# Two-layer stream step: up weights in one tile per 128 features, prepared two stages ahead, and the order of work at the two MLP ends

## The chip, the cores and the metric

The kernel runs on one core of a Trainium2 chip. The metric is device time in microseconds (us) of one execution; the median of several executions is compared, and the rows come from one execution that was recorded with the hardware profiler.

## The reference, cut to what matters

Two layers run over 1056 tokens (1024 of a new stream, 32 of a running one) of 1024 features; layer 0 mixes tokens with a gated recurrence, layer 1 with a short convolution. The change touches the two MLPs alone.

```python
def rmsnorm(x, g):
    return (x * lax.rsqrt(jnp.mean(x * x, axis=-1, keepdims=True) + EPS)) * g
...
    h = h + y                                  # y: the token mixer of layer i
    m = rmsnorm(h, norm_mlp[i])
    h = h + jnp.square(jax.nn.relu(m @ w_up[i])) @ w_down[i]     # 1024 -> 4096 -> 1024
return rmsnorm(h, norm_final), ...
```

## The kernel before, in words

**Numbers.** Activations lie with features on the 128 partitions and tokens in the free dimension. Every operand of a product, activation or weight, is split into a high part (a cast) and a low part (the difference), and a product is three matmuls on TensorE (PE): low times high, high times low, high times high (`mm3`, lines 107 to 110). Weights are fetched by SyncE's (SP) queue into a `raw` tile of 512 KB, cast to `whi` by ScalarE (ACT, L94) and subtracted to `wlo` by VectorE (DVE, L95). There are three raw, four `whi` and four `wlo` buffers. The residual stream is `hT`, eight tiles of 128 x 1056; the normalised input of an MLP is `xh`, `xl`, eight of each.

**One MLP** (`mlp`, L761). The 4096 hidden features are 16 chunks c of 256. `up(c)` takes two weight tiles, makes two halves j of 128 features in three groups of tokens (384, 384 and 288), 72 matmuls a half, and evacuates each half into a tile `u`: relu and scale on DVE (L788), square on ACT (L789). `sums(c)` makes from the two `u` the seven operand parts (B11, B22, Q1, Q2, T3, B21, T4) of a product of Strassen's kind. `down(c, b)` is one half-block of the down projection, for four of the eight tiles of `hT`: its weights are made by `wsums` (fetch, cast L717 and subtraction L718 of three blocks, four additions of weight blocks on GpSimd (POOL), L720, cast L721 and subtraction L722 of the four sums, so two pairs of `whi` and `wlo`); then come seven steps, each twice (p = 0, 1) six matmuls of 264 columns (L809), which accumulate in PSUM tiles a, b and c. A step's result is added to `hT` by DVE (L818); the first and the last step's is first copied out by ACT (L708) and then added once more by POOL (L709). The third and fifth steps accumulate further in tile a, so they wait until what it held has been read.

**Buffers.** `u`, operand parts and `hT` share one pool of 18 tiles (`ft`); PSUM has four tiles of two banks; there are four `st` tiles for the staged copies.

**The order.** The program is written as a list of stages: up(0), sums(0), up(1), down(0, 0), down(0, 1), sums(1), up(2) and so on. The weights of a stage are prepared (fetch, casts, sums) when the stage before it begins. A scheduler at build time turns the written order, the dependences and the free buffers into one order for each engine; on the chip each engine works in its order. In layer 0 the 16th chunk goes through `plain` (ordinary products, evacuated by L835 and the line below) behind down(14, 1); in layer 1 the last two chunks go through `groups` (products for three groups of tokens, 416 columns in the widest, evacuated by L860), so that the final norm can start early. Both read their activations from tiles of `xh` and `xl`, which the last `up` stages still need; so `split` (L180 and L181) fills them behind the last up projection, and only then comes the last `down`.

The stage list before is:

```python
        for c in range(n):                      # n = 15 in layer 0, 14 in layer 1
            stages.append(up(c))
            if c:
                stages += [down(c - 1, 0), down(c - 1, 1)]
            stages.append(lambda c=c: sums(c))
        stages += [up(c) for c in range(n, NFC)]
        rows = [(c, j) for c in range(n, NFC) for j in range(2)]
        stages.append(lambda: [split(k if last else 6 + k, U[c][j]) for k, (c, j) in enumerate(rows)])
        stages += [down(n - 1, 0), down(n - 1, 1)]
        stages += [groups()] if last else [plain(0), plain(1)]
```

Of the kernel before, what the change touches and what calls it, by code (L numbers as in the profile page):

```python
# [35 lines left out]
def trunk_kernel(  # L36
# [93 lines left out]
    def newps():  # L130
        return psum["new"]()
# [471 lines left out]
    def trio():  # L603

        a, b = pt(), pt()
        return a, [a[:, 0], a[:, 1], b[:, 0]]
# [154 lines left out]
    def mlp(layer, nrm, on_final, last):  # L761
        Wu, Wd = wg_up[layer], wg_down[layer]
        U, X = {}, {}
        two = lambda t: t[:, :768].rearrange("p (i c) -> p i c", i=2)
        sq = lambda t: nc.scalar.activation(t, t, AF.Square)

        def up(c):
            def run(wt):
                U[c] = []
                for j in range(2):  # L770
                    first = c == j == 0
                    a, pss = trio()
                    if first:
                        mm_rows(pss, wt, j, xsrc, nrm.scale)
                    else:
                        for g in range(3):
                            sl, n = gsl(g)
                            mm_block(pss[g], n, sl.start, wt, j, xsrc)
                    r = nrm.r
                    spare = last and (c, j) == (NFC - 1, 1)  # L780
                    u = mp.tile([P, NTOK], F32, tag="sq", name="ulast") if spare else ft("u")
                    for d, ps, sl in ((two(u), a[:, :, :384], slice(0, 768)), (u[:, 768:], pss[2][:, :288], slice(768, NTOK))):
                        if c == 0:
                            nc.scalar.activation(d, ps, AF.Relu)
                            nc.vector.tensor_tensor(u[:, sl], u[:, sl], r[:, sl], op=ALU.mult)
                        else:
                            rr = two(r) if sl.start == 0 else r[:, sl]
                            nc.vector.scalar_tensor_tensor(d, ps, 0.0, rr, op0=ALU.max, op1=ALU.mult)  # L788
                        nc.scalar.activation(u[:, sl], u[:, sl], AF.Square)  # L789
                    U[c].append(u)  # L790

            return lambda: wload(Wu, c), run

        def sums(c):
            X[c] = xsums(*U.pop(c))

        def down(c, b):
            def run(w):
                x = X[c]
                ps = [{}, {}]  # L800
                for i, (bank, f, g, start) in enumerate(STEPS):
                    for p in range(2):
                        if start:
                            ps[p][bank] = pt()
                        t = ps[p][bank]
                        (hi, lo), (xhi, xlo) = w(f, p), x[g]
                        for n, (wf, xf) in enumerate(((lo, xhi), (hi, xlo), (hi, xhi))):
                            for q in range(2):
                                nc.tensor.matmul(t[:, q, :QT], wf, xf[:, q * QT : (q + 1) * QT],  # L809
                                                 start=start and n == 0, stop=n == 2, skip_group_check=True)  # L810
                        v = t[:, :, :QT]
                        for r, h, op in TO[i]:
                            d = hT[4 * b + 2 * p + r][:, h * HALF : (h + 1) * HALF]
                            if i in STAGED:
                                st = mp.tile([P, HALF], F32, tag="st", name="st", bufs=4)
                                stage(d, st, v, op)
                            else:
                                nc.vector.tensor_tensor(q2(d), q2(d), v, op=op)  # L818

            return lambda: wsums(Wd[c, b]), run  # L820

        def plain(b):


            def run(wt):
                hi, lo = wt
                for m in range(4 * b, 4 * b + 4):
                    a, pss = trio()
                    cs = slice(m % 4 // 2 * P, (m % 4 // 2 + 1) * P)
                    for g in range(3):  # L830
                        sl, n = gsl(g)
                        for k in range(2):
                            t = BLK[(m % 2, k)]
                            mm3(pss[g][:, :n], hi[:, t, cs], lo[:, t, cs], xh[6 + k][:, sl], xl[6 + k][:, sl], k == 0, k == 1)
                    nc.vector.tensor_tensor(two(hT[m]), two(hT[m]), a[:, :, :384], op=ALU.add)  # L835
                    nc.vector.tensor_tensor(hT[m][:, 768:], hT[m][:, 768:], pss[2][:, :288], op=ALU.add)
                    if m < 6:
                        on_final(m)
                    elif m == 7:
                        on_final(6)  # L840
                        on_final(7)

            return lambda: wsplit(Wd[NFC - 1, b]), run

        def groups():

            n = NFC - 2

            def run(wts):
                for g in range(3):  # L850
                    c0, nt = FGROUPS[g]
                    sl = slice(c0, c0 + nt)
                    for m in range(KT):
                        ps = newps()[:, :nt]
                        cs = slice(m % 4 // 2 * P, (m % 4 // 2 + 1) * P)
                        for k in range(4):
                            hi, lo = wts[k // 2][m // 4]
                            t = BLK[(m % 2, k % 2)]
                            mm3(ps, hi[:, t, cs], lo[:, t, cs], xh[k][:, sl], xl[k][:, sl], k == 0, k == 3)
                        nc.vector.tensor_tensor(hT[m][:, sl], hT[m][:, sl], ps, op=ALU.add)  # L860
                        on_final(g, m)
# [170 lines left out]
    return np.ascontiguousarray(w.reshape(k // 512, 4, P, n // 256, 256).transpose(3, 0, 2, 1, 4))  # L1032


def _blocks(w):


    import numpy as np

    k, n = w.shape  # L1040
    t = w.reshape(k // 256, 2, P, n // 512, 2, 2, P)
    t = t.transpose(0, 3, 2, 5, 1, 4, 6)
    t = np.stack([t[:, :, :, 0, 0], t[:, :, :, 0, 1], t[:, :, :, 1, 1], t[:, :, :, 1, 0]], 3)
    return np.ascontiguousarray(t.reshape(k // 256, n // 512, P, 4, 256))


def _lay(inputs):
# [6 lines left out]
    return {  # L1054
        "x_t": np.ascontiguousarray(np.concatenate([a["x_prompt"][0], a["x_sample"][0]], 0).T),
        "vecs": np.ascontiguousarray(np.concatenate([cols(a[n]) for n in (
            "norm_mix", "norm_mlp", "norm_final", "g_norm_hgrn", "conv_w", "lb_hgrn", "state_conv")], 1)),
        "state_hgrn": np.ascontiguousarray(a["state_hgrn"]),
        "wg_in_hgrn": _grid(a["w_in_hgrn"][0]),
        "wg_out_hgrn": _grid(a["w_out_hgrn"][0]),  # L1060
        "wg_b_conv": _grid(wc[:, :D]),
        "wg_cu_conv": _grid(cu),
        "wg_out_conv": _grid(a["w_out_conv"][0]),
        "wg_up": np.stack([_grid(w) for w in a["w_up"]]),
        "wg_down": np.stack([_blocks(w) for w in a["w_down"]]),
    }

# [29 lines left out]
```

## Time and profile before

| | |
|---|---|
| median of 3 runs | 2478.2 us (2478.15 to 2479.04) |
| profiled execution | 2478.32 us, its span 2476.3 |
| mean granted clock of TensorE | 0.994 of full speed |
| busy, of the span | PE 2416.0 (98%), DVE 1601.4 (65%), ACT 779.9 (31%), POOL 772.3 (31%) |
| DMA | 122 MB, 49 GB/s |

The span is the stretch from the first to the last instruction; the profiled execution's own time is 2.0 us longer. PE is the engine that is almost always busy, so its idle time is what a reader looks for. The first sum-products of the two MLPs start at 668.1 us and 1775.6 us of the span.

### The profile page before, as it was taken

To read this page: it belongs to the slowest core of one execution; us is meant where nothing else is said; L and a number is where in the kernel's file an instruction comes from. 1 tells how busy PE (TensorE), PEld (TensorE's weight loads), DVE (VectorE), ACT (ScalarE), POOL (GpSimd) and SP (SyncE) were. 2 spreads that over 40 slices of the span, in tenths; PEclk is the share of its full clock that TensorE was granted. 3 is DMA by queue.
4 is the path that set the end of the run, shared out by engine and by line. 5 is a ranking of instruction groups with operands and counts; after the bars stand their busy time and mean duration, and the time that the engine had idled before them with its cause. 6 is when DMAs were issued, how large, how long until landed. Compare 5 with 4: busy or idle time off the path is not lost.

```text
span 2476.3 us, 39365 instructions
## 1 busy us (share of the span) xinstructions
PE 2416.0 (98%) x16548; PEld 2376.2 (96%) x16548; DVE 1601.4 (65%) x2384; ACT 779.9 (31%) x1275; POOL 772.3 (31%) x792
## 2 busy tenths in 40 slices
PE   8999999999999999999998999999999999999988
PEld 8999999989999999999998999999999999999987
DVE  8775757553776776767767533244776767767655
ACT  5121212132333333334334111123333333333334
POOL 3110101011253544535545000002244535544323
PEclk9999999999999999999999999999999999999999
DMA  4101010121111111111111111111111111111101
GB/s 149 38 29 47 21 55 21 55 107 35 35 52 43 60 43 43 52 43 52 44 43 60 36 50 52 35 52 45 41 44 43 52 43 53 42 43 60 52 26 71
DMA packets 35760, 121.99 MB, mean 49 GB/s; under 512 B 4336, under 2 KB 7552, under 8 KB 35584
## 3 DMA queue, kind: packets, MB, share of 16 engines
q1 hardware_dynamic: 33632, 113.58, 14.0%
q0 software_dynamic: 1952, 5.92, 0.6%
q8 instruction: 129, 2.11, 0.4%
q14 instruction: 47, 0.39, 0.0%
HBM read 114.09 MB, written 5.39 MB: 48 GB/s over the span
## 4 chain that ended last, share of the span: by engine, by line
PE 85%; DVE 6%; POOL 4%; ACT 3%; issue 3%; DMA 0%; DVEq 0%; SPq 0%; ACTq 0%; POOLq 0%
PE pb L809 18%; PE pb L108 16%; PE pb L109 15%; PE pb L110 15%; POOL raw L720 4%; PE pj L108 4%; PE pj L109 3%; PE pj L110 3%; DVE wlo L722 1%; ACT whi L721 1%; PE v L492 1%; PE v L493 1%; PE v L494 1%; DVE wlo L718 1%; DVE u L788 1%
## 5 line engine op out<-in xcount | busy, mean ns | idle before, releaser
L108 PE MATMUL pb<-xh,wlo 128*128 128x384 f32 (+2 forms) x2640 | 861.4, 326 | 4.3 <-DVE hT L835 4.3
L110 PE MATMUL pb<-xh,whi 128*128 128x384 f32 (+2 forms) x2640 | 854.2, 324 | 0.0
L109 PE MATMUL pb<-xl,whi 128*128 128x384 f32 (+2 forms) x2640 | 854.0, 323 | 0.0
L108 PEld LDWEIGHTS pb<-xh,wlo 128*128 128x128 f32 x2640 | 497.1, 188 | 9.1 <-issue 2.6
L110 PEld LDWEIGHTS pb<-xh,whi 128*128 128x128 f32 x2640 | 497.2, 188 | 0.5
L109 PEld LDWEIGHTS pb<-xl,whi 128*128 128x128 f32 x2640 | 497.3, 188 | 0.3
L709 POOL TENSOR_TENSOR hT<-hT,st 128x528 f32<-128x528 f32 x232 | 404.1, 1768 | 251.3 <-ACT st L708 251.3
L818 DVE TENSOR_TENSOR hT<-hT,pb 128x528 f32<-128x528 f32 x580 | 374.1, 694 | 45.2 <-PE pb L809 41.1
L720 POOL TENSOR_TENSOR raw<-raw 128x256 f32<-128x256 f32 x232 | 205.8, 887 | 510.8 <-DVE wlo L718 497.2
L94 ACT CAST whi<-raw 128x1024 fp32r<-128x1024 f32 (+1 forms) x143 | 149.1, 1045 | 423.6 <-PE pb L110 265.3
L809 PE MATMUL pb<-B,whi 128*128 128x264 f32 x1392 | 226.8, 285 | 0.0
L95 DVE TENSOR_TENSOR wlo<-raw,whi 128x1024 fp32r<-128x1024 f32 (+1 forms) x143 | 182.6, 1280 | 59.6 <-ACT whi L94 59.1
L809 PEld LDWEIGHTS pb<-B,whi 128*128 128x128 f32 x1392 | 193.2, 189 | 0.0
L108 PE MATMUL pj<-xh,wlo 128*128 128x384 f32 (+1 forms) x536 | 177.7, 332 | 6.3 <-ACT xh L183 6.3
L109 PE MATMUL pj<-xl,whi 128*128 128x384 f32 (+1 forms) x536 | 173.5, 324 | 0.0
L110 PE MATMUL pj<-xh,whi 128*128 128x384 f32 (+1 forms) x536 | 173.1, 323 | 0.0
L708 ACT COPY st<-pb 128x528 f32<-128x528 f32 x232 | 136.1, 601 | 117.1 <-PE pb L809 109.7
L788 DVE SCALAR_TENSOR_TENSOR u<-pb,nr 128x768 f32<-128x768 f32 x118 | 80.5, 701 | 137.8 <-PE pb L110 137.8
L809 PE MATMUL pb<-T,whi 128*128 128x264 f32 x928 | 152.2, 286 | 0.0
L809 PE MATMUL pb<-Q,whi 128*128 128x264 f32 x928 | 150.8, 284 | 0.0
L809 PE MATMUL pb<-B,wlo 128*128 128x264 f32 x696 | 141.8, 285 | 0.0
L722 DVE TENSOR_TENSOR wlo<-raw,whi 128x1024 fp32r<-128x1024 f32 x58 | 71.9, 1239 | 107.5 <-ACT whi L721 107.5
(239 smaller groups left out, 3484.8 us busy)
## 6 DMA issues: line engine op xcount, KB each, us to landing
raw<-in_wg_up_dram SPq DMA_DIRECT2D x64, 512.0 KB, 3.6
raw<-in_wg_down_dram SPq DMA_DIRECT2D x64, 512.0 KB, 3.5
raw<-in_wg_in_hgrn_dram SPq DMA_DIRECT2D x31, 512.0 KB, 4.3
raw<-in_wg_cu_conv_dram SPq DMA_DIRECT2D x16, 512.0 KB, 3.5
xk<-in_x_t_dram SPq DMA_DIRECT2D x8, 528.0 KB, 8.2
hT<-in_x_t_dram POOLq DMA_DIRECT2D x8, 528.0 KB, 6.7
raw<-in_wg_out_hgrn_dram SPq DMA_DIRECT2D x8, 512.0 KB, 4.0
raw<-in_wg_b_conv_dram SPq DMA_DIRECT2D x8, 512.0 KB, 3.5
```

The lines of the kernel that those rows point to most:

```text
L94: nc.scalar.copy(hi, raw)
L95: nc.vector.tensor_tensor(lo, raw, hi.bitcast(F32), op=ALU.subtract)
L108: nc.tensor.matmul(ps, wlo, ah, start=start, stop=False)
L109: nc.tensor.matmul(ps, whi, al, start=False, stop=False)
L110: nc.tensor.matmul(ps, whi, ah, start=False, stop=stop)
L708: nc.scalar.copy(q2(st), v)
L709: nc.gpsimd.tensor_tensor(d, d, st, op=op)
L720: nc.gpsimd.tensor_tensor(raw[:, d], raw[:, d], raw[:, o], op=ALU.add)
L722: nc.vector.tensor_tensor(lo2, raw, hi2.bitcast(F32), op=ALU.subtract)
L788: nc.vector.scalar_tensor_tensor(d, ps, 0.0, rr, op0=ALU.max, op1=ALU.mult)
L809: nc.tensor.matmul(t[:, q, :QT], wf, xf[:, q * QT : (q + 1) * QT], start=start and n == 0, stop=n == 2, skip_group_check=True)
L818: nc.vector.tensor_tensor(q2(d), q2(d), v, op=op)
```

## The change

An up projection's weights come in one tile of 512 KB for each half of 128 features (all eight row blocks of the input) in place of two tiles of 256 features by half the rows; the host lays them out so (`_rows`). `up(c)` becomes two stages, `up(c, 0)` and `up(c, 1)`. Weights are prepared two stages ahead in place of one. In layer 0 the two `split` calls stand between down(14, 0) and down(14, 1). In layer 1 down(13, 0) and down(13, 1) stand ahead of the two halves of up(15), and the operands of `groups` go by `gsplit` into `ft` tiles of their own (gh and gl) and not into `xh` and `xl`; in its first group of tokens `groups` multiplies the first three operands of four outputs before it takes the fourth operand.

```diff
@@ mlp
-        def up(c):
+        def up(c, j):
+            m = 2 * c + j
...
+            def prep():
+                rows = lambda t: t.rearrange("p a (b c) -> p (a b) c", c=P)
+                return [rows(t) for t in wsplit(Wu[m])]
...
+        G = []
+
+        def gsplit(u):
+            h, l = [fp.tile([P, NTOK], F32R, tag="ft", name=t) for t in ("gh", "gl")]
+            nc.scalar.copy(h, u)
+            nc.vector.tensor_tensor(l, u, h.bitcast(F32), op=ALU.subtract)
+            G.append((h, l))
+
@@ groups
-                    for m in range(KT):
-                        ps = newps()[:, :nt]
+                    pss = {}
+                    order = [(m, k) for m in range(KT) for k in range(4)]
+                    if g == 0:
+                        order = [(m, k) for m in range(4) for k in range(3)] + [(m, 3) for m in range(4)] + order[16:]
...
-                            mm3(ps, hi[:, t, cs], lo[:, t, cs], xh[k][:, sl], xl[k][:, sl], k == 0, k == 3)
...
+                        gh, gl = G[k]
+                        mm3(pss[m], hi[:, t, cs], lo[:, t, cs], gh[:, sl], gl[:, sl], k == 0, k == 3)
@@ stages
-            stages.append(up(c))
+            stages += [up(c, 0), up(c, 1)]
...
-        stages += [up(c) for c in range(n, NFC)]
-        rows = [(c, j) for c in range(n, NFC) for j in range(2)]
-        stages.append(lambda: [split(k if last else 6 + k, U[c][j]) for k, (c, j) in enumerate(rows)])
-        stages += [down(n - 1, 0), down(n - 1, 1)]
-        stages += [groups()] if last else [plain(0), plain(1)]
+        stages += [up(n, 0), up(n, 1)]
+        if last:
+            stages += [down(n - 1, 0), down(n - 1, 1)]
+            stages.append(lambda: [gsplit(U[n][j]) for j in range(2)])
+            for j in range(2):
+                stages.append(up(n + 1, j))
+                stages.append(lambda j=j: gsplit(U[n + 1][j]))
+            stages.append(groups())
+        else:
+            stages.append(down(n - 1, 0))
+            stages.append(lambda: [split(6 + j, U[n][j]) for j in range(2)])
+            stages += [down(n - 1, 1), plain(0), plain(1)]
...
-        ready = {0: work[0][0]()}
-        k = 0
+        ready = [work[0][0](), work[1][0]()]
...
-            if k + 1 < len(work):
-                ready[k + 1] = work[k + 1][0]()
-            s[1](ready.pop(k))
-            k += 1
+            if len(ready) < len(work):
+                ready.append(work[len(ready)][0]())
+            s[1](ready[work.index(s)])
```

Line numbers shift a little: L788, L789, L818, L835 and L860 become L787, L788, L821, L838 and L878; those up to 761 stay. Three places show how the instructions move. The names end in a running number, and `u`, `pb`, `nr`, `hT` and `raw` are the up result, PSUM, the norm's scale, the residual stream and the fetched weights.

The first place is DVE in a regular cycle of the first MLP, from the evacuation of an up projection into the first half-block of the down projection. Before:

```order
L788 SCALAR_TENSOR_TENSOR u_7686<-pb_7612,nr_6124 128x768
L788 SCALAR_TENSOR_TENSOR u_7686<-pb_7613,nr_6124 128x288
L788 SCALAR_TENSOR_TENSOR u_7765<-pb_7691,nr_6124 128x768
L744 TENSOR_TENSOR B11_8020<-u_7686,B11_8020 128x528
L718 TENSOR_TENSOR wlo_7772<-raw_7770,whi_7771 128x768
L788 SCALAR_TENSOR_TENSOR u_7765<-pb_7692,nr_6124 128x288
L818 TENSOR_TENSOR hT1_5399<-hT1_5399,pb_7804 128x528
L818 TENSOR_TENSOR hT3_5575<-hT3_5575,pb_7812 128x528
L722 TENSOR_TENSOR wlo_7774<-raw_7770,whi_7773 128x1024
L818 TENSOR_TENSOR hT0_5319<-hT0_5319,pb_7784 128x528
L818 TENSOR_TENSOR hT2_5493<-hT2_5493,pb_7794 128x528
```

With the change:

```order
L787 SCALAR_TENSOR_TENSOR u_7686<-pb_7612,nr_6118 128x768
L787 SCALAR_TENSOR_TENSOR u_7686<-pb_7613,nr_6118 128x288
L718 TENSOR_TENSOR wlo_7693<-raw_7691,whi_7692 128x768
L787 SCALAR_TENSOR_TENSOR u_7779<-pb_7705,nr_6118 128x768
L744 TENSOR_TENSOR B11_8020<-u_7686,B11_8020 128x528
L787 SCALAR_TENSOR_TENSOR u_7779<-pb_7706,nr_6118 128x288
L722 TENSOR_TENSOR wlo_7695<-raw_7691,whi_7694 128x1024
L821 TENSOR_TENSOR hT1_5399<-hT1_5399,pb_7810 128x528
L821 TENSOR_TENSOR hT3_5575<-hT3_5575,pb_7818 128x528
L821 TENSOR_TENSOR hT0_5319<-hT0_5319,pb_7790 128x528
L821 TENSOR_TENSOR hT2_5493<-hT2_5493,pb_7800 128x528
```

L718 and L722, which prepare the second half-block's weights, move ahead of the evacuation of the second up half and ahead of all four additions of the half-block; before, L722 stood between them.

The second place is ACT in the same cycle. Before:

```order
L789 ACTIVATE u_7765<-u_7765 128x768
L717 CAST whi_7771<-raw_7770 128x768
L708 COPY st_7791<-pb_7784 128x528
L789 ACTIVATE u_7765<-u_7765 128x288
L708 COPY st_7801<-pb_7794 128x528
L721 CAST whi_7773<-raw_7770 128x1024
L94 CAST whi_7897<-raw_7896 128x1024
```

With the change:

```order
L788 ACTIVATE u_7686<-u_7686 128x768
L717 CAST whi_7692<-raw_7691 128x768
L788 ACTIVATE u_7686<-u_7686 128x288
L743 CAST B11_8020<-u_7686 128x528
L788 ACTIVATE u_7779<-u_7779 128x768
L721 CAST whi_7694<-raw_7691 128x1024
L788 ACTIVATE u_7779<-u_7779 128x288
L708 COPY st_7797<-pb_7790 128x528
L708 COPY st_7807<-pb_7800 128x528
L94 CAST whi_7785<-raw_7784 128x1024
```

The cast L717 now follows the first half's square, and L721 stands ahead of the last square and of both staged copies, where it stood behind them.

The third place is DVE at the end of the second MLP, around the last half-blocks. Before, with `ulast` the last up result:

```order
L788 SCALAR_TENSOR_TENSOR ulast_22387<-pb_22313,nr_16106 128x768
L181 TENSOR_TENSOR xl0_81<-u_22136,xh0_73 128x1056
L788 SCALAR_TENSOR_TENSOR ulast_22387<-pb_22314,nr_16106 128x288
L181 TENSOR_TENSOR xl1_82<-u_22215,xh1_74 128x1056
L181 TENSOR_TENSOR xl2_83<-u_22308,xh2_75 128x1056
L718 TENSOR_TENSOR wlo_22402<-raw_22400,whi_22401 128x768
L181 TENSOR_TENSOR xl3_84<-ulast_22387,xh3_76 128x1056
L818 TENSOR_TENSOR hT1_5399<-hT1_5399,pb_22434 128x528
L818 TENSOR_TENSOR hT3_5575<-hT3_5575,pb_22442 128x528
L818 TENSOR_TENSOR hT0_5319<-hT0_5319,pb_22414 128x528
L722 TENSOR_TENSOR wlo_22404<-raw_22400,whi_22403 128x1024
L818 TENSOR_TENSOR hT2_5493<-hT2_5493,pb_22424 128x528
```

With the change:

```order
L95 TENSOR_TENSOR wlo_22238<-raw_22236,whi_22237 128x1024
L821 TENSOR_TENSOR hT2_5493<-hT2_5493,pb_22328 128x528
L853 TENSOR_TENSOR gl_22473<-u_22138,gh_22472 128x1056
L95 TENSOR_TENSOR wlo_22356<-raw_22354,whi_22355 128x1024
L821 TENSOR_TENSOR hT5_5751<-hT5_5751,pb_22380 128x528
L821 TENSOR_TENSOR hT7_5927<-hT7_5927,pb_22388 128x528
```

The four L181 of the `split` calls and the weight preparation stood ahead of the last sum-product's additions; now the first `gsplit` subtraction (L853) and the weights of up(15) stand among the additions of the two half-blocks, ahead of those for hT5 and hT7.

## Rows read from the trace of the kernel before

**Rows 1.** The page's busy table: busy us, share of the span, instructions of each engine.

```profile
PE 2416.0 (98%) x16548; PEld 2376.2 (96%) x16548; DVE 1601.4 (65%) x2384; ACT 779.9 (31%) x1275; POOL 772.3 (31%) x792
```

**Rows 2.** Waits of PE, whole span: us in total, times, longest us.

```profile
PE pb L809 <- DVE hT L818: 31.6, 29, 5.3
...
PE pb L108 <- DVE hT L835: 4.3, 2, 2.4
...
PE pb L809 <- ACT st L708: 1.0, 1, 1.0
```

**Rows 3.** Waits of PE in 630:1300, 1300:1310, 1700:2380 and 2380:2400.

```profile
PE pb L809 <- DVE hT L818: 12.1, 14, 0.9
...
PE pb L809 <- DVE hT L818: 2.7, 1, 2.7
...
PE pb L809 <- DVE hT L818: 11.4, 13, 0.9
...
PE pb L809 <- DVE hT L818: 5.3, 1, 5.3
```

**Rows 4.** Timeline of one cycle: start, us, instruction, [idle before and its releaser].

```profile
703.84 1.31 DVE L788 SCALAR_TENSOR_TENSOR u<-pb,nr 128x768 f32<-128x768 f32 x2
704.82 1.18 ACT L789 ACTIVATE u<-u 128x768 f32<-128x768 f32 x2 [1.64 <-DVE u L788]
...
711.44 0.81 ACT L717 CAST whi<-raw 128x768 fp32r<-128x768 f32 x1
...
712.29 0.96 DVE L718 TENSOR_TENSOR wlo<-raw,whi 128x768 fp32r<-128x768 f32 x1 [1.02 <-ACT whi L717]
...
712.56 0.30 PE L110 MATMUL pb<-xh,whi 128*128 128x288 f32 x1
...
712.69 0.40 PE L809 MATMUL pb<-B,wlo 128*128 128x264 f32 x2
...
713.33 3.18 POOL L720 TENSOR_TENSOR raw<-raw 128x256 f32<-128x256 f32 x4 [15.76 <-DVE wlo L718]
...
713.62 0.60 ACT L708 COPY st<-pb 128x528 f32<-128x528 f32 x1 [1.36 <-PE pb L809]
...
714.11 0.45 ACT L789 ACTIVATE u<-u 128x288 f32<-128x288 f32 x1
...
715.08 1.44 DVE L818 TENSOR_TENSOR hT<-hT,pb 128x528 f32<-128x528 f32 x2 [1.47 <-PE pb L809]
...
715.62 0.40 PE L809 MATMUL pb<-Q,wlo 128*128 128x264 f32 x2
...
716.54 1.05 ACT L721 CAST whi<-raw 128x1024 fp32r<-128x1024 f32 x1 [1.50 <-POOL raw L720]
...
717.63 1.26 DVE L722 TENSOR_TENSOR wlo<-raw,whi 128x1024 fp32r<-128x1024 f32 x1 [1.11 <-ACT whi L721]
...
719.56 0.51 PE L809 MATMUL pb<-T,wlo 128*128 128x264 f32 x2 [0.85 <-DVE hT L818]
```

**Rows 5.** Chain of waits, three half-blocks' matmuls: start, us, engine, line, count.

```profile
1257.40 14.84 PE pb L809 x120
...
1304.00 16.19 PE pb L809 x120
...
2394.32 16.55 PE pb L809 x114
```

**Rows 6.** Windows: us, busy (x) PE, PEld, DVE, ACT, POOL, granted clock, DMA, GB/s.

```profile
2394.00:2396.00 2.00, 1.69 (x7) 1.69 (x8) 2.00 (x4) 0.00 (x0) 0.00 (x0) 0.50 0.59 180
```

**Rows 7.** Timeline of POOL at the first MLP's end.

```profile
1296.01 4.98 POOL L720 TENSOR_TENSOR raw<-raw 128x256 f32<-128x256 f32 x4 [9.10 <-DVE wlo L718]
```

**Rows 8.** Timeline of DVE at the second MLP's end.

```profile
2379.69 1.26 DVE L181 TENSOR_TENSOR xl<-u,xh 128x1056 fp32r<-128x1056 f32 x1 [0.89 <-ACT xh L180]
```

**Rows 9.** Timeline of DVE in `groups`: additions of two outputs, one after the other.

```profile
2417.72 0.59 DVE L860 TENSOR_TENSOR hT<-hT,pb 128x416 f32<-128x416 f32 x1 [0.41 <-PE pb L110]
...
2419.99 0.59 DVE L860 TENSOR_TENSOR hT<-hT,pb 128x416 f32<-128x416 f32 x1 [0.41 <-PE pb L110]
```

More of the change, by code (lines that the diff above doesn't have):

```diff
@@ L765, in mlp @@
         sq = lambda t: nc.scalar.activation(t, t, AF.Square)
-        def up(c):
+        def up(c, j):
+            m = 2 * c + j
             def run(wt):
[L769 to L774, printed above, removed]
-                    else:
[L776 to L792, printed above, removed]
@@ new lines, in run @@
+                hi, lo = wt
+                a, pss = trio()
+                ks = [(k, g) for k in range(KT) for g in range(3)] if m == 0 else [(k, g) for g in range(3) for k in range(KT)]
+                for i, (k, g) in enumerate(ks):
+                    sl, n = gsl(g)
+                    if m == 0 and i == 3 * (KT - 1):
+                        nrm.scale()
+                    mm3(pss[g][:, :n], hi[:, k], lo[:, k], xh[k][:, sl], xl[k][:, sl], k == 0, k == KT - 1)
+                r = nrm.r
@@ new lines, in run @@
+                u = ft("u")
+                for d, ps, sl in ((two(u), a[:, :, :384], slice(0, 768)), (u[:, 768:], pss[2][:, :288], slice(768, NTOK))):
+                    if c == 0:
+                        nc.scalar.activation(d, ps, AF.Relu)
+                        nc.vector.tensor_tensor(u[:, sl], u[:, sl], r[:, sl], op=ALU.mult)
+                    else:
+                        rr = two(r) if sl.start == 0 else r[:, sl]
+                        nc.vector.scalar_tensor_tensor(d, ps, 0.0, rr, op0=ALU.max, op1=ALU.mult)
+                    nc.scalar.activation(u[:, sl], u[:, sl], AF.Square)
@@ L794, in sums @@
+                U.setdefault(c, []).append(u)
+            def prep():
+                rows = lambda t: t.rearrange("p a (b c) -> p (a b) c", c=P)
+                return [rows(t) for t in wsplit(Wu[m])]
+            return prep, run
         def sums(c):
@@ L852, in run @@
                     sl = slice(c0, c0 + nt)
-                    for m in range(KT):
-                        ps = newps()[:, :nt]
-                        cs = slice(m % 4 // 2 * P, (m % 4 // 2 + 1) * P)
-                        for k in range(4):
-                            hi, lo = wts[k // 2][m // 4]
-                            t = BLK[(m % 2, k % 2)]
-                            mm3(ps, hi[:, t, cs], lo[:, t, cs], xh[k][:, sl], xl[k][:, sl], k == 0, k == 3)
-                        nc.vector.tensor_tensor(hT[m][:, sl], hT[m][:, sl], ps, op=ALU.add)
-                        on_final(g, m)
+                    pss = {}
+                    order = [(m, k) for m in range(KT) for k in range(4)]
+                    if g == 0:
+                        order = [(m, k) for m in range(4) for k in range(3)] + [(m, 3) for m in range(4)] + order[16:]
+                    for m, k in order:
+                        if k == 0:
+                            pss[m] = newps()[:, :nt]
+                        cs = slice(m % 4 // 2 * P, (m % 4 // 2 + 1) * P)
+                        hi, lo = wts[k // 2][m // 4]
+                        t = BLK[(m % 2, k % 2)]
+                        gh, gl = G[k]
+                        mm3(pss[m], hi[:, t, cs], lo[:, t, cs], gh[:, sl], gl[:, sl], k == 0, k == 3)
+                        if k == 3:
+                            nc.vector.tensor_tensor(hT[m][:, sl], hT[m][:, sl], pss[m], op=ALU.add)
+                            on_final(g, m)
             return lambda: [[wsplit(Wd[n + c, b]) for b in range(2)] for c in range(2)], run
@@ L1032, in _grid, with _rows @@
     return np.ascontiguousarray(w.reshape(k // 512, 4, P, n // 256, 256).transpose(3, 0, 2, 1, 4))
+def _rows(w):
+    import numpy as np
+    k, n = w.shape
+    return np.ascontiguousarray(w.reshape(k // P, P, n // P, P).transpose(2, 1, 0, 3).reshape(n // P, P, k // 256, 256))
 def _blocks(w):
@@ L1063, in _lay @@
         "wg_out_conv": _grid(a["w_out_conv"][0]),
-        "wg_up": np.stack([_grid(w) for w in a["w_up"]]),
+        "wg_up": np.stack([_rows(w) for w in a["w_up"]]),
         "wg_down": np.stack([_blocks(w) for w in a["w_down"]]),
```

## The prediction

> **What bounds the kernel now.** The busy table comes first: TensorE (PE) works 2416.0 us, 98% of the span of 2476.3, and no other engine passes 65% [rows 1]. An edit that keeps the matmuls, as this one does, can win only what PE loses: idle time, and time at its lower clock. So the next view is the table of PE's waits. Its largest line is the sum-product matmul of L809 waiting for the VectorE (DVE) addition of L818, 31.6 us in 29 waits, the longest 5.3; then L809 waiting for the staged copy of L708, 1.0, and L108 waiting for L835 of `plain`, 4.3 in two [rows 2]. Cut by stretch, the 29 fall apart: 14 of 12.1 us in the first MLP, 13 of 11.4 in the second, each at most 0.9, and one long one at each MLP's end, 2.7 and 5.3 [rows 3].
>
> The timeline of one cycle shows where the 0.87 (23.5 / 27) comes from. A cycle is an up projection of one chunk, two half-blocks of sum-products (seven steps each) and the sums. The last up matmul starts at 712.56, the first sum-product at 712.69, the third step at 715.62, so a step takes about 1.47. The weights of the second half-block are prepared while the first runs: cast L717 at 711.44, subtraction L718, four GpSimd (POOL) additions of 3.18 in all, cast L721 at 716.54, subtraction L722 until 718.89. In DVE's order L722 stands ahead of the L818 additions that free bank a, so PE's fifth step starts at 719.56 after 0.85 idle, where 718.71 was possible [rows 4]. What ends last is the weight preparation, through a queue; DVE is not short of time.
>
> The long stalls cost twice. In the chain of waits a half-block's 120 matmuls that went undisturbed took 14.84, those behind the 2.7 us stall 16.19, and 114 behind the 5.3 us stall 16.55 [rows 5]. The window from 2394.00 has a granted clock of 0.50, that is 1.2 of 2.4 GHz, after PE had stood still for over 5 us [rows 6]. At the full pace 114 matmuls need 114 x 14.84 / 120 = 14.10, so the lower clock costs 16.19 - 14.84 = 1.35 and 16.55 - 14.10 = 2.45.
>
> **The change part by part.** Matmuls, weight transfers, casts and subtractions keep their number and size: a chunk still has two weight tiles of 512 KB, now one for each half, and four `gsplit` pairs stand for four `split` pairs. Nothing is priced there; SP's queue issues the same transfers, one stage earlier, and a raw tile stays held by its own preparation alone.
>
> *The regular cycle, 27 times.* The second half-block's weights are now made during the second up half. Let the first sum-product again start at 712.69. L717 follows the first half's evacuation and squares, which in the old trace (for the second half) begin at 703.84 and 704.82 and take 1.31 and 1.18 [rows 4]; with 0.81 for L717 and 0.96 for L718 the latter ends near 707.3 or 708. The POOL additions take 3.18 where POOL is alone, 4.98 in the slowest row I read [rows 4, 7]: done by 710.5 to 713. L721 then wants the hi buffer that the second up half's last matmul still reads, which ends at 712.56 + 0.30 = 712.86. So L721 runs from 712.9 to 713.95 instead of from 716.54.
>
> Two things now stand behind it. On ACT: the last Square (0.45) and the staged copies (0.60 each). The first copy, which wants step 1's output, ends at 713.95 + 0.45 + 0.60 = 715.0 at the latest, 714.6 if the Square slips ahead; the third step, which accumulates into the same bank, starts at 715.62. A slack of 0.6 or more. On DVE: L722, 713.95 to 715.2, then the two additions of bank b (1.44 for both, to 716.65), then the first of bank a, 0.72, to 717.4. The fifth step wants it at 718.71: a slack of 1.3. So the bubble goes with nothing in its place: 27 x 0.87 = **23.5 us**. What is late next is nothing on PE's path in the first half-block. In the second, DVE has what it had before without its L718 and L722; L94 and L95 of the next up half move in there, one tile at a time instead of two, beside 10 us of matmuls in each half-block.
>
> *The end of the first MLP.* The stall of 2.7 had L722 behind POOL additions of 4.98 that started at 1296.01 [rows 7]. Now these weights are made during the last up half, and the two `split` calls come behind down(14,0). One split copy (1.05, by the same shape as L721) can stand ahead of the staged copy there: 3.0 us after the first matmul against a need at 2.93, so I charge 0.1. Gain: 2.7 and the 1.35 of lower clock. `plain` keeps its 4.3 us of waits [rows 2], as its matmuls and evacuation are the same.
>
> *The end of the second MLP.* Before, the four `split` pairs follow the last up projection, and PE waits 5.3 for sum-products whose weights queue behind them (the first L181 at 2379.69, 1.26 each) [rows 3, 8]. Now down(13) runs ahead of up(15), where its order is that of a regular cycle. That removes 5.3, the 1.0 of the staged copy and 2.45 of clock: **with the first MLP's end 2.7 + 5.3 + 1.0 = 9.0 of waits, and 1.35 + 2.45 = 3.8 of clock.** New is a wait of `gl`: the eight hT, seven operand parts, two u and gh fill all 18 buffers, so the first gl must wait for a part that the second half-block's first step frees, 1.62 into it. Behind it on DVE stand a weight subtraction and the addition for hT5: 1.62 + 1.26 (as [rows 8]) + 1.26 + 0.70 = 4.85, while the fourth step wants it at 3 x 1.47 = 4.40. Charge: 0.45. The last up half now goes straight into `groups`, whose fourth operand needs a cast 1.05, Square 0.45, copy 1.05 and subtraction 1.26 after the last matmul: some 4 us. The cover is the reordered first part: 12 products of 3 matmuls with 416 columns, as many as three whole sums before, and one of those takes 2.27 (2417.72 to 2419.99) [rows 9]: 6.8 us. So it costs nothing; without that cover it would cost 4 and the clock's fall after it.
>
> **The sum.** 23.5 + 9.0 + 3.8 = 36.3 off, 0.1 + 0.45 added: net 35.75. The durations come from one execution of 2478.3, its span and 2.0 around it; the median of the three runs shown is 2478.2, so 0.1 separates the two. 2478.3 - 35.75 = **2442.6**.
>
> **A rule against it.** The 27 waits are one gap that repeats. The trace releases it by an addition that stands behind L722, and L722 by POOL's sums of weights; by these rows an earlier start cures it [rows 3, 4]. The Trainium skill, page "Perfetto Trace Analysis", section "Optimization Strategy", says that a gap repeating on the engine that should be saturated can mean too few buffers for the next tile; by that rule alone nothing would be won in the cycle, since the change adds no weight buffer. The rival is C below.
>
> **The rivals.** *B: part of the bubble stays.* For it: four hi buffers hold exactly one cycle, and POOL has staged additions of its own; if its sums take 4.98 each time and DVE reaches them late, L721 starts near 714 and some 0.3 us stays in each cycle. 27 x 0.3 = 8.1: **2450.7**. Against: with L718 done near 708, even 4.98 ends by 713, within 0.2 of the buffer's release [rows 4, 7].
>
> *C: the repeating gap stays or moves.* If the fourth set's cast is released late enough that L722 still ends behind the additions' need, only the ends gain: 9.0 + 3.8 - 0.55 = 12.25, **2466.1**. Against: the buffer is free at 712.86, 3.7 us ahead of where L721 starts now [rows 4]. The rule of the Trainium skill above is this case.
>
> *D: slower.* L721 now stands ahead of both staged copies on ACT. If it starts as late as before, at 716.54, the copy of bank a ends near 716.54 + 1.05 + 0.45 + 0.60 = 718.6, and the third step loses 2.9 us of 715.62 onwards. 28 cycles x 2.9 = 81 against 36.3: about **2523**, more with the clock's fall. The stalls begin when L721 starts after 713.5; the change breaks even at 36.3 / 28 = 1.3 more, **714.8**. For it: ACT works in order, and what L721 waits for (POOL) has the longest chain. Against: that chain has ended by 713 even with the slowest additions, and the break-even asks for 1.8 more.
>
> *E: the change doesn't do what it says* (the built order keeps the old places) is excluded by the rows of the order shown with the change.
>
> **How the numbers follow.** The forecast 0.72 (own range 2438 to 2448: the charges of 0.55 may be 0 or some 3 with a fall of the clock; the clock after `plain`'s stalls may give or take 1.3; each 0.1 us left in a cycle is 2.7), B 0.13, C 0.08, D 0.05, the rest between these. 2438 to 2455 takes in the forecast and B and leaves out C, D and the tails, under 2 in 10. A difference of 0.2%, 5 us, is about what a measurement of this kernel can tell from no change. A, B and C are faster by more than that: 0.91, with 0.02 for mixtures cut off; within it 0.04, cycles with L721 near the break-even; slower 0.05, D.
>
> **What would show it.** Right: PE's wait for the additions (L821 in the changed lines) falls from 31.6 us to under 2; L721 starts directly behind the last up matmul, its copies follow at 0.6 or more ahead of the third step; no window at 0.50 of the clock at the two ends; the two waits for `plain` stay. B shows waits of 0.3 at the fifth or third step in most cycles; C shows about 27 waits of 0.8 with a release by L722 or a buffer; D shows L809 waiting for L708 in every cycle. It would be wrong too if matmuls took longer each: the 120 of a half-block must stay at 14.84.

## The result, and the profile after

The changed kernel took 2444.94 us (median of 4 runs, 2442.30 to 2445.74) against 2478.18 for the kernel before in the same comparison: a ratio of 0.9865, 95% interval 0.9848 to 0.9882. Forecast were 2442.6 and 2438 to 2455, so the time lies in the range, 2.3 above the number. The profiled execution took 2445.29, its span 2443.6, 32.7 less than the span before.

The busy table and two lines of the table of PE's waits, whole span, answer to [rows 1, 2]:

```profile
PE 2412.2 (99%) x16548; PEld 2373.4 (97%) x16548; DVE 1635.0 (67%) x2384; ACT 775.8 (32%) x1275; POOL 744.1 (30%) x792
...
PE pb L108 <- DVE hT L838: 3.4, 2, 2.3
PE pb L812 <- DVE hT L821: 3.3, 2, 2.3
```

The 32.6 us that L809 waited are now 3.3 in two waits, one at each MLP's end (1.0 and 2.3); in the regular cycles the table has none. PE's busy time fell by 3.8 with the same matmuls; by the rows of the chain 2.3 of that is clock at the two ends (1.35 + 2.45 before, 1.48 now, below). The weight loads (PEld), which run just ahead of their matmuls, have a table of waits of their own, and there 29 waits are left, 27 of them of 0.2, one in each cycle:

```profile
PEld pb L812 <- DVE hT L821: 8.8, 29, 2.5
```

The timeline of the cycle that answers to [rows 4] (start, us, instruction, idle before and releaser):

```profile
704.94 0.82 ACT L717 CAST whi<-raw 128x768 fp32r<-128x768 f32 x1
705.79 0.96 DVE L718 TENSOR_TENSOR wlo<-raw,whi 128x768 fp32r<-128x768 f32 x1 [1.27 <-ACT whi L717]
706.83 3.19 POOL L720 TENSOR_TENSOR raw<-raw 128x256 f32<-128x256 f32 x4 [9.90 <-DVE wlo L718]
711.93 0.40 PE L812 MATMUL pb<-B,wlo 128*128 128x264 f32 x2
712.18 1.05 ACT L721 CAST whi<-raw 128x1024 fp32r<-128x1024 f32 x1 [1.40 <-PE pb L110]
713.26 1.23 DVE L722 TENSOR_TENSOR wlo<-raw,whi 128x1024 fp32r<-128x1024 f32 x1 [0.68 <-ACT whi L721]
713.48 1.08 ACT L708 COPY st<-pb 128x528 f32<-128x528 f32 x2
717.78 0.40 PE L812 MATMUL pb<-T,wlo 128*128 128x264 f32 x2
726.67 0.30 PEld L812 LDWEIGHTS pb<-B,wlo 128*128 128x128 f32 x2 [0.19 <-DVE hT L821]
```

L717 starts 7.0 us ahead of the first sum-product, where before it started 1.25 ahead. L721 waits no more for POOL but for the last up matmul (L110), which frees its buffer, and starts 0.25 behind the first sum-product, where before it was 3.85. The fifth step comes 5.85 behind the first, without a wait. The last row is the wait of the weight loads: in the second half-block one waits 0.19, which the table of PE's waits doesn't show. The addition that it waits for stands behind a weight subtraction that takes 2.08 while POOL works:

```profile
722.31 6.17 POOL L709 TENSOR_TENSOR hT<-hT,st 128x528 f32<-128x528 f32 x4 [5.33 <-ACT st L708]
723.92 2.08 DVE L95 TENSOR_TENSOR wlo<-raw,whi 128x1024 fp32r<-128x1024 f32 x1 [1.23 <-ACT whi L94]
```

The chain of waits, half-blocks of after (start, us, matmuls):

```profile
712.09 20.69 PE pb L812 x168
756.02 20.71 PE pb L812 x168
...
1773.77 6.10 PE pb L812 x48
...
2346.81 7.58 PE pb L812 x48
```

A cycle is 756.02 - 712.09 = 43.93, where the chain of before has 44.82 in this place (719.56 to 764.38): 0.89 less, 0.87 forecast. At the second MLP's end, 48 matmuls take 7.58 where they took 6.10 undisturbed: 1.48 of lower clock. DVE there, and the matmul and the clock behind it (timeline, then a row of windows as [rows 6]):

```profile
2341.67 2.21 DVE L853 TENSOR_TENSOR gl<-u,gh 128x1056 fp32r<-128x1056 f32 x1 [1.13 <-PE pb L812]
2343.80 2.34 DVE L95 TENSOR_TENSOR wlo<-raw,whi 128x1024 fp32r<-128x1024 f32 x1
2346.81 0.59 PE L812 MATMUL pb<-B,wlo 128*128 128x264 f32 x1 [2.27 <-DVE hT L821]
2348.00:2350.00 2.00, 2.00 (x11) 2.00 (x10) 1.38 (x3) 0.00 (x0) 0.00 (x0) 0.50 0.44 174
```

This is the place where the prediction charged 0.45, with both subtractions at 1.26 [rows 8]. They take 2.21 and 2.34. POOL works in that time:

```profile
2340.14 7.17 POOL L709 TENSOR_TENSOR hT<-hT,st 128x528 f32<-128x528 f32 x4 [5.32 <-ACT st L708]
```

The first MLP's end has the same picture, L181 at 2.15 and L95 at 2.35 beside four additions of L709, and PE's wait of 1.0 behind them:

```profile
1293.52 2.15 DVE L181 TENSOR_TENSOR xl<-u,xh 128x1056 fp32r<-128x1056 f32 x1
1295.59 2.35 DVE L95 TENSOR_TENSOR wlo<-raw,whi 128x1024 fp32r<-128x1024 f32 x1
```

### The profile page after: what moved, and what is told of

It is laid out like the page before. It is cut to its first block, busy times and chain, and to the rows that moved or that the text cites. A ratio compares the mean times of both kernels' runs of the same rounds, so it can differ in the third digit from the quotient of the medians.

```text
span 2443.6 us, 39446 instructions
## 1 busy us (share of the span) xinstructions
PE 2412.2 (99%) x16548; PEld 2373.4 (97%) x16548; DVE 1635.0 (67%) x2384; ACT 775.8 (32%) x1275; POOL 744.1 (30%) x792
## 4 chain that ended last, share of the span: by engine, by line
PE 97%; DVE 2%; ACT 0%; issue 0%; DMA 0%; DVEq 0%; SPq 0%; ACTq 0%
PE pb L812 25%; PE pb L108 17%; PE pb L109 17%; PE pb L110 17%; PE pj L108 4%; PE pj L109 4%; PE pj L110 3%; PE v L492 1%; PE v L493 1%; PE v L494 1%; PE aps L385 1%; PE aps L390 1%; PE ops L427 1%; PE ups L402 1%; PE ops L426 1%; PE aps L388 0%
## 5 line engine op out<-in xcount | busy, mean ns | idle before, releaser
L108 PE MATMUL pb<-xh,wlo 128*128 128x384 f32 (+1 forms) x2544 | 829.3, 326 | 3.4 <-DVE hT L838 3.4
L109 PE MATMUL pb<-xl,whi 128*128 128x384 f32 (+1 forms) x2544 | 822.4, 323 | 0.0
L110 PE MATMUL pb<-xh,whi 128*128 128x384 f32 (+1 forms) x2544 | 822.4, 323 | 0.0
L709 POOL TENSOR_TENSOR hT<-hT,st 128x528 f32<-128x528 f32 x232 | 373.2, 1635 | 404.0 <-ACT st L708 404.0
L108 PEld LDWEIGHTS pb<-xh,wlo 128*128 128x128 f32 x2544 | 478.6, 188 | 8.2 <-issue 2.5
L110 PEld LDWEIGHTS pb<-xh,whi 128*128 128x128 f32 x2544 | 478.7, 188 | 0.4
L109 PEld LDWEIGHTS pb<-xl,whi 128*128 128x128 f32 x2544 | 478.7, 188 | 0.2
L821 DVE TENSOR_TENSOR hT<-hT,pb 128x528 f32<-128x528 f32 x580 | 383.4, 697 | 9.1 <-PE pb L812 0.8
L95 DVE TENSOR_TENSOR wlo<-raw,whi 128x1024 fp32r<-128x1024 f32 (+1 forms) x143 | 202.6, 1420 | 67.4 <-ACT whi L94 66.9
L110 PE MATMUL pj<-xh,whi 128*128 128x384 f32 (+1 forms) x536 | 173.1, 323 | 0.0
L787 DVE SCALAR_TENSOR_TENSOR u<-pb,nr 128x768 f32<-128x768 f32 x120 | 82.2, 704 | 124.0 <-PE pb L110 124.0
L708 ACT COPY st<-pb 128x528 f32<-128x528 f32 x232 | 133.0, 600 | 80.6 <-PE pb L812 68.9
L788 ACT ACTIVATE u<-u 128x768 f32<-128x768 f32 (+1 forms) x128 | 81.7, 642 | 161.3 <-DVE u L787 156.4
```

What stands on the lines that cost most here:

```text
L95: nc.vector.tensor_tensor(lo, raw, hi.bitcast(F32), op=ALU.subtract)
L108: nc.tensor.matmul(ps, wlo, ah, start=start, stop=False)
L109: nc.tensor.matmul(ps, whi, al, start=False, stop=False)
L110: nc.tensor.matmul(ps, whi, ah, start=False, stop=stop)
L708: nc.scalar.copy(q2(st), v)
L709: nc.gpsimd.tensor_tensor(d, d, st, op=op)
```

## The experiments

Three questions were open. Which part of the change makes the gain? Why were the weights late: order, look-ahead or buffers? Why do the subtractions take nearly twice as long?

**e1 and e2: look-ahead or tile.** e1 takes the look-ahead out of the change; e2 puts it alone into the kernel before.

```diff
-        ready = [work[0][0](), work[1][0]()]
+        ready = [work[0][0]()]
```

> The changed kernel with weights prepared one stage ahead again; tiles of one half and both reordered ends stay. If the look-ahead makes the cycle's gain, 27 gaps of about 0.87 us return: 2444.9 + 23.5 = about 2468, with some 28 waits of L812 for the additions of L821. If the tile of one half does it by itself (weights released sooner), the waits stay away: about 2445.

Measured: 2442.61 (2441.39 to 2443.84), ratio 0.9859 to before (0.9844 to 0.9874). The rival held. The cycle is that of the change: chain rows of 20.69 for 168 matmuls, 43.94 apart, no PE wait in any cycle, and ACT's and DVE's instructions in the cycle in the same order. With the tile of one half the look-ahead adds nothing.

```diff
-        ready = {0: work[0][0]()}
+        ready = {0: work[0][0](), 1: work[1][0]()}
...
-            if k + 1 < len(work):
-                ready[k + 1] = work[k + 1][0]()
+            if k + 2 < len(work):
+                ready[k + 2] = work[k + 2][0]()
```

> The kernel before with weights prepared two stages ahead, and nothing else; an up projection still holds two tiles for both halves. If both parts are needed, the second half-block's cast still waits for the buffers that the whole up projection reads, so L721 starts as late as before (3.8 us after the first sum-product) and the gaps stay: 2476 to 2480. If the look-ahead is enough, the gaps go: 2478 - 23.5 = about 2455.

Measured: 2497.33 (2496.82 to 2499.11), ratio 1.0081 (1.0066 to 1.0096). The gaps stayed, as expected, but the kernel became slower, which was not. PE's waits in 630 to 1270, and the chain, with a cycle of 45.52:

```profile
PE pb L809 <- DVE hT L818: 12.1, 14, 0.9
```

```profile
685.68 4.64 PE pb L809 x36
720.45 10.74 PE pb L809 x84
731.22 4.64 PE pb L809 x36
```

The old gap is there (12.1 in 14), and each second half-block has new small waits of weight loads, 0.18 for L708's copy at 725.07 and 0.25 for an addition at 731.22. A cycle is 0.70 longer than before, and 27 of them make 18.9, nearly all of the loss of 19. So with the old tile the look-ahead does change the order; what made that order was not taken apart.

**e3: the old order at both ends**, with tile and look-ahead of the change; the operands of `groups` are in `xh` and `xl` again, and `groups` is in plain order.

```diff
-            stages += [down(n - 1, 0), down(n - 1, 1)]
-            stages.append(lambda: [gsplit(U[n][j]) for j in range(2)])
...
+        stages += [up(c, j) for c in range(n, NFC) for j in range(2)]
+        rows = [(c, j) for c in range(n, NFC) for j in range(2)]
+        stages.append(lambda: [split(k if last else 6 + k, U[c][j]) for k, (c, j) in enumerate(rows)])
+        stages += [down(n - 1, 0), down(n - 1, 1)]
+        stages += [groups()] if last else [plain(0), plain(1)]
```

> The changed kernel with the stages at the two ends in the order of before: all split calls behind the last up projection into xh and xl, the last half-blocks behind them, groups in plain order. By the prediction's sum the ends' gains go back: 2.7 + 1.35 of the first MLP and 5.3 + 1.0 + 2.45 of the second, less the waits of 1.0 and 2.3 that the change has there: about 2453. Rival: those waits were the late weights too, and two stages ahead cures them in either order: about 2445.

Measured: 2444.92 (2443.33 to 2446.02), ratio 0.9868 (0.9853 to 0.9883): the time of the change. The rival held. The first end has 0.8 of waits in two, the second 1.6 and 0.5: no more than the new order has. Before, the 2.7 and 5.3 were the late weights, too.

**e5: the tile alone**, in the kernel before: `up(c, j)` with its own tile of 512 KB, one stage ahead, old ends.

> The kernel before with the up tile of one half and nothing else: one stage ahead, both ends in the old order, xh and xl as the operands of groups. Theory after e1 to e3: what delayed the second half-block's weights was a hi/lo buffer held by the up projection to its end, and a tile of one half gives it back after the first half; look-ahead and order at the ends add nothing, so about 2443 to 2445. Rival: look-ahead and new order each cure the ends, and one of them is needed: 2450 or more, with waits of some us around 1300 and 2350.

Measured: 2442.01 (2441.76 to 2443.70), ratio 0.9858 (0.9843 to 0.9872). The tile alone gives the whole gain; the rest of the change has no gain that these runs can tell. Its casts stand as in the change:

```profile
705.37 0.82 ACT L717 CAST whi<-raw 128x768 fp32r<-128x768 f32 x1
712.62 1.05 ACT L721 CAST whi<-raw 128x1024 fp32r<-128x1024 f32 x1 [1.41 <-PE pb L110]
```

**e6: a buffer in place of the tile.** If the tile helps because it gives back a hi/lo pair after half an up projection, one more pair should do the same in the kernel before.

```diff
+        if own:
+            raw = ws.tile([P, 4, 256], F32, tag="raw", name="raw", bufs=3)
+            hi, lo = [mp.tile([P, NTOK], F32R, tag=t, name=n)[:, :1024].rearrange("p (a b) -> p a b", b=256)
+                      for t, n in (("sq", "hio"), ("acc", "loo"))]
+        else:
+            raw, hi, lo = wtiles()
```

> The kernel before with one more hi/lo pair, for the three blocks (L717, L718 of before) of the second half-block's weights in all cycles but the last of each MLP; the pair lies in tiles that stand idle in that time. Up tiles of both halves, one stage ahead, old ends. If a missing buffer made the gap, these casts and the POOL sums start long before the first sum-product, and the 27 gaps of 0.87 go: 2478.3 - 23.5 = about 2455, the two waits at the ends staying. If the gap comes from the tile's shape, the transfers or the order on DVE, it stays: 2478.

Measured: 2474.57 (2473.14 to 2475.49), ratio 0.9987 (0.9978 to 0.9997). Neither number: the time stayed near that of before, but the gap did not stay where it was. The chain and the wait in the cycle:

```profile
712.35 10.23 PE pb L814 x84
728.43 5.40 PE pb L814 x42
```

```profile
728.43 0.51 PE L814 MATMUL pb<-B,wlo 128*128 128x264 f32 x2 [0.74 <-DVE hT L823]
```

The fifth step of the first half-block waits no more. The first cast for the second half-block's weights now starts 20 us earlier, into the tile of its own:

```profile
689.68 0.84 ACT L722 CAST hio<-raw 128x768 fp32r<-128x768 f32 x1
```

With a buffer the old gap is closed, so the missing buffer had made it. A new gap of 0.74 stands in the second half-block, where the next weights' subtraction has moved in, at the slow pace:

```profile
723.97 2.04 DVE L723 TENSOR_TENSOR wlo<-raw,whi 128x768 fp32r<-128x768 f32 x1 [1.02 <-ACT whi L722]
...
726.54 1.22 DVE L749 TENSOR_TENSOR B<-u,B 128x528 fp32r<-128x528 f32 x1
```

**e4 and e9: POOL silenced, the order kept.** Both leave out most of POOL's staged additions in one stretch (8 of 528 columns are left) and keep the order on ACT and DVE as it is: e4 in the changed kernel, in the last two half-blocks of each MLP; e9 in e6, for the last step of each first half-block and the first step of each second one.

```diff
+        if short:
+            d, st = d[:, :8], st[:, :8]
         nc.gpsimd.tensor_tensor(d, d, st, op=op)
```

> The changed kernel, but the staged POOL additions (L709) of the last two sum-product half-blocks of each MLP work on 8 of 528 columns, so most of these additions are left out; the order on PE, ACT and DVE is unchanged. Theory: DVE's subtractions with two SBUF operands take longer while POOL adds. Then at the second MLP's end the subtraction of gl takes 1.26 and not 2.21, the weight subtraction behind it 1.22 and not 2.34, and PE's wait there falls from 2.3 to about 0.2; at the first MLP's end the 2.15 and 2.35 become 1.26 and 1.22 and the wait of 1.0 goes; with the clock about 2440.5. Rival: the durations have another cause (ACT's or TensorE's traffic, transfers): all of these stay, 2445.

Measured: 2441.62 (2440.55 to 2442.93), and at the second end, then at the first (DVE):

```profile
2341.01 1.26 DVE L855 TENSOR_TENSOR gl<-u,gh 128x1056 fp32r<-128x1056 f32 x1 [1.13 <-PE pb L814]
2342.18 1.22 DVE L95 TENSOR_TENSOR wlo<-raw,whi 128x1024 fp32r<-128x1024 f32 x1
...
1293.95 1.25 DVE L181 TENSOR_TENSOR xl<-u,xh 128x1056 fp32r<-128x1056 f32 x1
...
1295.29 1.22 DVE L95 TENSOR_TENSOR wlo<-raw,whi 128x1024 fp32r<-128x1024 f32 x1
```

The same instructions at the same places take 1.26, 1.22, 1.25 and 1.22 where they took 2.21, 2.34, 2.15 and 2.35, and PE's two waits shrink to 0.2 in all. The theory held to the hundredth in the durations.

> The kernel of e6, but the POOL additions (L709) of the last step of each first half-block and of the first step of each second one work on 8 of 528 columns, so most of these additions are left out; the order on PE, DVE and ACT is that of e6. Theory: e6 has closed the old gap in the first half-block, and its 26 waits of about 0.7 are new ones in the second, because the weight subtraction L723 and the operand subtraction L749 take 2.04 and 1.22 beside POOL's additions where 0.96 and 0.70 are their quiet times: 1.6 us of slack returns, the waits go, 2474.6 - 18.7 = about 2456. Rival: the waits are the order on DVE and not its speed: 2474.

Measured: 2448.32 (2447.57 to 2449.78), ratio 0.9878 (0.9862 to 0.9895), 26.3 less than e6 where 18.7 were expected. In the cycles no wait is left, neither of PE nor of its weight loads, and the chain shows why it is more:

```profile
712.20 20.48 PE pb L816 x168
755.92 20.48 PE pb L816 x168
```

A cycle is 43.72, less than the change's 43.93, and its 168 matmuls take 20.48 where the change has 20.69: the wait of 0.19 in the change's second half-block is gone as well. That wait had stood in the changed kernel's first profile, in the rows of the weight loads.

**e7: no cover.** `groups` in plain order (the two lines of `if g == 0` left out).

> The changed kernel with groups in plain order: the first output takes all four operands before the second begins. By the prediction the fourth operand is some 4 us late and costs that and a fall of the clock: 2448 to 2450. By the changed kernel's trace it is ready 3.5 us after the last up matmul, of which three operands of one output cover 1.7: a wait of 1.8, and 2447. Rival: the wait falls where it is made good later: 2445.

Measured: 2443.99 (2443.30 to 2444.48), and no wait in `groups`. The rival's number held, but not its reason: no wait is made that would have to be made good. PE's built order has a cover of its own: it still puts the second output's first products ahead of the first one's last ones with the fourth operand. The scheduler does it unasked.

**e8: the ends mended in the code.** The last first half-block of each MLP adds its first and last step from PSUM.

```diff
-                            if i in STAGED:
+                            if i in STAGED and (b or c < (NFC - 3 if last else NFC - 2)):
```

> The changed kernel, but the last first half-block of each MLP adds its first and last step straight from PSUM on DVE (0.70 each) in place of the copy and POOL's addition. Without POOL at work the subtractions behind it take 1.2 to 1.3, and the order puts gl behind the additions: both waits at the ends (1.0 and 2.3) and the fall of the clock behind the second go, 2445 - 1.0 - 2.3 - 1.4 = about 2440 to 2441. Rival: the additional work on DVE makes a new wait of the same size: 2445.

Measured: 2443.97 (2442.62 to 2444.84): no difference from the change that can be told. The second end is free of waits, but the first has two now:

```profile
PE pb L812 <- DVE hT L821: 2.3, 2, 1.2
```

Three subtractions and four additions follow each other on DVE there, and L95 still takes 2.34 beside the next half-block's POOL additions. The rival held at that end, the theory at the other.

**e10 and e11: towards a faster version.** e10 takes the better piece for each end; e11 takes POOL's work away where e9 had shown its price.

```diff
-            stages.append(down(n - 1, 0))
             stages.append(lambda: [split(6 + j, U[n][j]) for j in range(2)])
-            stages += [down(n - 1, 1), plain(0), plain(1)]
+            stages += [down(n - 1, 0), down(n - 1, 1), plain(0), plain(1)]
...
-        ready = [work[0][0](), work[1][0]()]
+        ready = [work[0][0]()]
```

> The changed kernel with the pieces that had the smaller waits where they were run alone: one stage ahead, the first MLP's end in the old order (split calls ahead of both last half-blocks), the second MLP's end in the new order. If the pieces add up: e1 without waits at the second end, less its 1.4 and 4.6 at the first and with 0.7 and 2.7 of e5 there: 2442.6 - 2.6 = about 2440. Rival: the order moves elsewhere and gives waits of the same size: 2442 to 2443.

Measured: 2441.87 (2441.49 to 2442.68), ratio 0.9851 (0.9836 to 0.9866). Nearer to the rival's 2442.

```diff
-                            if i in STAGED:
+                            if i in STAGED and (b, i) != (0, 6):
```

> The kernel of e10, and in all first half-blocks the last step's result is added straight from PSUM on DVE (0.70 each), without the copy on ACT and POOL's addition. Theory: the changed kernel still loses 0.2 in each cycle (168 matmuls of two half-blocks take 20.69, in e9 20.47, with a wait of 0.19 of the weight load for an addition behind a subtraction that takes 2.08 beside POOL); with POOL silent there that subtraction takes about 1.2 to 1.5, and two more additions of 0.70 fit into 1.2 us in which DVE now waits. Cycle 43.93 to 43.72: 27 x 0.2 = 5.5, with 2441.9 for e10 about 2436 to 2437. Rival: DVE's added 1.4 us makes a wait of its own in each cycle: 2442 or more.

Measured: 2433.84 (2433.38 to 2435.34), ratio 0.9823 (0.9810 to 0.9836): 44 us below the kernel before and 11 below the change. DVE, and the chain:

```profile
722.80 1.93 DVE L821 TENSOR_TENSOR hT<-hT,pb 128x528 f32<-128x528 f32 x3
724.65 1.22 DVE L95 TENSOR_TENSOR wlo<-raw,whi 128x1024 fp32r<-128x1024 f32 x1
```

```profile
712.90 20.44 PE pb L812 x168
756.58 20.45 PE pb L812 x168
```

Two more additions stand in front of L95, L95 takes 1.22 in place of 2.08, and the cycle is 43.68. Over e10 that is 0.25 in each of 27 cycles, 6.7 of the 8.0 us; the rest was not taken apart. The theory held, with more than it asked for.

## Why the prediction was right, and where it was not

**The size of the cycle's gain** held: 0.87 forecast; by the mean of the cycles 0.90 in the first MLP (44.82 to 43.92) and 0.88 in the second (44.78 to 43.90), together 14 x 0.90 + 13 x 0.88 = 24.0 against 23.5. L721 directly behind the last up matmul, its two copies ahead of the third step, the fifth step without a wait: each was forecast and is in the rows. Of the size a part is luck, for two terms that the prediction lacks cancel. The weight load ahead of the old fifth step waited longer than the matmul (before):

```profile
719.56 0.30 PEld L809 LDWEIGHTS pb<-T,wlo 128*128 128x128 f32 x2 [1.07 <-DVE hT L818]
```

So some 1.1 was lost in a cycle, and 0.2 is still lost in the second half-block, which the prediction put at nothing with L95 moving in there. e11, without either, has a cycle 1.14 shorter than before (44.82 to 43.68). The prediction also reads the rows at 703.84 and 704.82 as the second half's evacuation; by the order shown with the change they are the first half's, and the times taken from them stand.

**Its cause** was given wrongly in one step. The prediction read the wait from its end (addition behind L722, L722 behind POOL, POOL behind L718) and took the earlier preparation for the cure. It did not ask what had held L717 until 711.44. Before, the first of the up projection's two tiles is read for the last time by the twelfth matmul of the third group of tokens:

```profile
710.96 0.29 PE L110 MATMUL pb<-xh,whi 128*128 128x288 f32 x1
```

It ends at 711.25, and L717 starts 0.19 behind it, when ACT is through with a Square. This row alone leaves it open whether the buffer or ACT's order held the cast. e2 (look-ahead alone: gaps stay), e5 (tile alone: gaps go) and e6 (one more pair: this gap goes) answer: L717 lacked a hi/lo buffer, which the up projection's tile held until its last reader in the second half. The Trainium skill, page "Perfetto Trace Analysis", section "Optimization Strategy", which was set aside by the row's releaser, names this cause: no room for the next tile, with buffer count and tile sizes as what to look at. The runs agree: the gap of 0.87 goes with the other cut of the tile (e5) and with one more pair (e6). Rival C took only the count from it, and its consequence, that nothing could be gained without a buffer, fell: a tile that is given back earlier closes the gap as a buffer does. That the sum came out in spite of the wrong cause is luck too: it adds up waits, whatever cures them, and the same terms would have stood for the look-ahead alone, which took 2497.33 (e2).

**The ends.** 9.0 of waits and 3.8 of clock were put down to the new order there. The old waits did go, but e3 and e5 show that the old order, with early weights, is as good. The cover in `groups`, priced at 4 us if it were missing, would not have cost that: the scheduler makes one in any case (e7).

**The mis-sized terms** are the charges of 0.1 and 0.45. Measured: 1.0, 2.3 and 1.48 of clock behind the latter, 4.2 more than charged. The 1.0 came from DVE, too, and not from the copy on ACT for which 0.1 was charged. The step that failed is "1.62 + 1.26 + 1.26 + 0.70": both subtractions at a price from a row in which POOL stood still, while POOL's four staged additions fall into that very stretch. With 2.21 and 2.34 the same sum gives 6.87 against the need at 4.40, 2.47; PE waited 2.27. With 0.5 more in the cycles and the two waits for `plain` 0.9 shorter this makes 33.0; the span is 32.7 shorter, where 35.75 were forecast. Two of the prediction's own signs of being right did not come: L821's waits are 3.3 and not under 2, and a window at 0.50 of the clock stands at the second end.

**The rivals.** B stated a wait of 0.3 in each cycle: one of 0.2 was there, at the fourth step of the second half-block and not where B put it, and it comes from a DVE subtraction beside POOL's staged additions, not from POOL's sums. D did not come up: L721 starts 0.25 behind the first sum-product, and 0.8 would have been allowed; its price is written as 28 cycles of 2.9, where its own rows give 27 of 3.0, the same 81.

## What to carry to other kernels

Follow a wait to the first instruction that starts late, not to the last one that ends it, and ask which buffer that one needs and who reads it last: a tile of the same size, cut so that it is released earlier, closed the same gap as an additional buffer, and here without the new gap that the buffer brought (2442.01 against 2474.57). Price an instruction by a row in which the same neighbours are at work, not by its quiet time. Where a pattern repeats, compare the period with that of the best variant, and read the waits of the weight loads beside PE's: waits of 0.2 in every cycle show only there and cost 6 us here.

## What the runs showed of the hardware

A DVE subtraction of two SBUF operands (128 x 1024) took 1.22 with POOL silent and 2.08 to 2.35 beside POOL's additions of 128 x 528. POOL's additions took 1.42 each (2.83 for two) while DVE added from PSUM, and 1.79 on average in the stretch with the subtractions (7.17 for four). DVE's additions with one operand in PSUM (L821) took 0.69 to 0.71 in all 580 cases. Two of POOL's additions beside them, in the changed kernel:

```profile
714.14 2.83 POOL L709 TENSOR_TENSOR hT<-hT,st 128x528 f32<-128x528 f32 x2 [4.12 <-ACT st L708]
```

e4 shows it as cause: POOL's work taken away, order kept, and the subtractions return to 1.22 to 1.26. The Trainium skill, page "SBUF — State Buffer", section "Who interferes with whom", says that a DVE instruction with two SBUF inputs contends with a GpSimd instruction that reads SBUF, and that one with at most one such input, outside the 2-port modes, does not. These rows agree on both points.
